# Loading and multiplying the last expert's gate and up rows ahead of the preceding expert's down rows

## The chip, the cores and the metric

One NeuronCore of one Trainium2 chip runs the kernel. The metric is the device time of one execution in microseconds (us); three executions of the kernel before have a median of 1208.63 us (1207.80 to 1209.83). A core has a matrix engine (TensorE, "PE" in the profile, its weight loads "PEld"), a vector engine (VectorE, "DVE"), a scalar engine (ScalarE, "ACT"), a general engine (GpSimd, "POOL") and a queue that issues transfers (SyncE, "SP"). Each engine works through a queue of its own; semaphores make one wait for another.

## The reference

One layer of a trunk: three parallel mixers, then an expert-choice mixture of experts, then a final RMSNorm. The change lies in the last two:

```python
def expert_choice_ffn(h, w_router, w_gate, w_up, w_down):
    b, n, d = h.shape
    cap = CAPACITY_FACTOR * n // N_EXPERTS
    aff = jax.nn.softmax((h @ w_router).astype(jnp.float32), axis=-1)
    gate, idx = lax.top_k(jnp.swapaxes(aff, 1, 2), cap)
    bidx = jnp.arange(b)[:, None, None]
    xe = h[bidx, idx]
    hid = jax.nn.silu(jnp.einsum('becd,edf->becf', xe, w_gate)) * jnp.einsum('becd,edf->becf', xe, w_up)
    ye = jnp.einsum('becf,efd->becd', hid, w_down) * gate[..., None].astype(h.dtype)
    return jnp.zeros_like(h).at[bidx, idx].add(ye)
...
    return rms_norm(x, g_final)
```

There are 512 tokens of 1024 channels and 16 experts. Each expert takes 64 tokens through a gate matrix, an up matrix (both 1024 x 1024) and a down matrix (1024 x 1024), all in float32: 12 MB of weights for each expert.

## The kernel before

**Order of work.** The helper class at lines 61 to 69 keeps the instructions of TensorE, VectorE, ScalarE and GpSimd in program order wherever `pinned[0]` is true. Line 1328 sets it and nothing clears it before line 1692, so through all the experts and the tail each of these engines works in the order in which the code names the instructions.

**Weights.** The expert weights come as chunks of 1 MB: chunk b (0 to 3) of a matrix holds the rows of steps k = 2b and 2b+1 of the products. The list `chunks` (lines 1106 to 1112) fixes the order of loading: for each expert e, first chunk 0 of gate and up of expert e+1, then the four down chunks of e, then chunks 1 to 3 of gate and up of e+1. Below, G15.2 is chunk 2 of the gate matrix of expert 15, U is up and D is down; the last two experts are e = 14 and e = 15. `fetch` (line 1114) issues the next chunk on SP into a free one of 18 buffers; `use` (line 1137) returns a buffer to the free list at the second step of a chunk. The products take the chunks in the order in which they were loaded. One chunk of the 18 is loaded as two halves (line 1131), and so is the very last chunk, D15.3.

**One expert** (lines 1574 to 1639). At the start of iteration e the gate and up products of e stand in two PSUM banks (`og[e]`). They are copied out (`gu`, one half on ScalarE, one on VectorE), TensorE turns them (8 transposes), ScalarE takes the Silu (`sgl`) and VectorE multiplies (`hid`). Between these, TensorE has steps 0 and 1 of the gate and up products of the next expert (`gate_up`, line 1536, eight matmuls a step). Then come the down products (line 1599, 8 steps of 4 matmuls), their weighting (`tt`, on VectorE) and the splitting of the result into a high and a low part (`yh` on ScalarE, `yl` on VectorE, two of each). Then steps 2 to 7 of the next expert's gate and up products.

**Putting tokens back.** Experts go back to their tokens in pairs: `slot_rows` (line 1458) makes four one-hot tiles on VectorE, `slots` (line 1511) turns them with four transposes and three copies on ScalarE into `OT`, and `scatter` multiplies. For the last pair (14 and 15) the one-hots are made at step 2 and turned at step 3 of `gate_up(15, k)`, and the products are left to the tail. `carry` (line 1532) brings the accumulated stream of one token tile and half into a PSUM bank by a product with the identity, so that the last pair's products can be added there: four of these lie at steps 3, 4, 5 and 6 of `gate_up(15, k)` (`EARLY`, line 1546), two behind the down products of expert 15.

**Tail** (lines 1643 to 1692). `last_scatter` adds the last pair to the four token tiles. Six of the eight halves stand in PSUM (carried): ScalarE squares and sums them (`ss3`). Two halves, of tiles 2 and 3, are added on VectorE and squared by `own_square`. The reciprocal root goes in steps on GpSimd (tile 0, then tiles 2 and 3 together) or on VectorE with one power on GpSimd (tile 1), and `put` scales the tile and writes it out.

Of the kernel before, what the change touches and what calls it, by code (L numbers as in the profile page):

```python
# [49 lines left out]
def kernel(ctx, tc, x, c, cctx_x, c_ctx, w_mod, b_mod, g_mix, g_ffn, w_in, decay, ret_gn, w_ret,  # L50
# [20 lines left out]
    def dap(t, offset, ap):  # L71
        return bass.AP(tensor=t.tensor, offset=t.offset + offset, ap=ap)
# [17 lines left out]
    def u8(shape, dtype=F32, name="u8"):  # L90
        return U8p.tile(list(shape), dtype, name=name, tag="u8")
# [32 lines left out]
    def small(shape, name, bufs=1):  # L124
        return keep.tile(list(shape), F32, name=name, tag=name, bufs=bufs)
# [976 lines left out]
    def gate_chunks(e, b0, b1):  # L1102
        for b in range(b0, b1):
            chunks.extend([("G", e, b), ("U", e, b)])

    gate_chunks(0, 0, KT // 2)
    for e in range(NE):
        if e + 1 < NE:
            gate_chunks(e + 1, 0, AHEAD // 2)
        chunks.extend(("D", e, b) for b in range(KT // 2))  # L1110
        if e + 1 < NE:
            gate_chunks(e + 1, AHEAD // 2, KT // 2)

    def fetch(most=99):
        while free and len(loaded) < len(chunks) and most:
# [342 lines left out]
    def slot_rows(e0):  # L1458
        oh = h2(F32R, "oh", (P, TT, P))
        for t in range(TT):  # L1460
            one_hot(oh[:, t, :], t, e0, 2)
        return oh
# [48 lines left out]
    def slots(oh):  # L1511
        o = px()
        for t in range(TT):
            PE.transpose(o[:, t * P:(t + 1) * P], f32(oh[:, t, :]), ident)
        OT = [h2(F32R, name="OT") for _ in range(2)]
        A.activation(OT[0], o, AF.Copy)
        A.activation(OT[1][0:64], o[64:128], AF.Copy)
        A.activation(OT[1][64:128], o[0:64], AF.Copy)
        return OT

# [11 lines left out]
    def carry(t, dh, bank):  # L1532
        Z[t][dh] = bank()
        mm(Z[t][dh], ident, acc(t, slice(dh * 512, dh * 512 + 512)), True, False)

    def gate_up(e, k):
        if k == 0:
            og[e] = [pa(), pa()]
        w = (use("G", e, k), use("U", e, k))
        for f in range(2):  # L1540
            for s_ in range(2):
                mm(og[e][f][64 * s_:64 * s_ + 64, :], xe(k, e), w[s_][:, f * 512:(f + 1) * 512], k == 0, k == KT - 1)
        fetch()

    Z = [[None, None] for _ in range(TT)]
    EARLY = {3: (0, 0, pa), 4: (0, 1, pa), 5: (3, 0, OC), 6: (1, 0, px)}

    ohs = h2(name="ohs", shape=(P, TT, CAP))
    xe0 = h2(name="xe0", shape=(P, KT, CAP))
# [24 lines left out]
    for e in range(NE):  # L1574
        last, par, nx = e == NE - 1, e % 2, e + 1
        gu = [h2(name="gu") for _ in range(2)]
        A.activation(gu[0], og[e][0], AF.Copy)
        V.tensor_copy(gu[1], og.pop(e)[1])
        if not last:
            gate_up(nx, 0)  # L1580
        hid = h2(name="hid", shape=(P, KT, CAP))
        for f in range(2):
            o = px()
            for j in range(4):
                PE.transpose(o[:, j * P:(j + 1) * P], gu[f][:, ch(j)], ident)
            ov = o.rearrange("p (j s) -> p j s", j=4)
            sgl = h2(name="sgl", shape=(P, 4, CAP))
            A.activation(sgl, ov[:, :, 0:CAP], AF.Silu)
            V.tensor_tensor(hid[:, 4 * f:4 * f + 4, :], sgl, ov[:, :, CAP:], op=OP.mult)
        if not last:  # L1590
            gate_up(nx, 1)
        if par and not last:
            oh = slot_rows(e - 1)
        if not par and not last and nx < NE - 1:
            g_ = gather(nx // 2 + 1)
            next(g_)
            next(g_)
        o = px()
        for f in range(KT):
            w = use("D", e, f)  # L1600
            for dh in range(2):
                g = dh ^ par
                mm(o[64 * g:64 * g + 64, :], hid[:, f, :], w[:, dh * 512:dh * 512 + 512], f == 0, f == KT - 1)
            fetch()
        if par == 0:
            Y[e] = [[h2(F32R, name="yy") for _ in range(2)] for _ in range(2)]
        tt = h2(name="tt")
        V.scalar_tensor_tensor(tt, o, gcol[:, e:e + 1], m5[par], op0=OP.mult, op1=OP.mult)
        for g in range(2):
            dh = g ^ par  # L1610
            sl = slice(64 * g, 64 * g + 64)
            yh, yl = Y[e - par]
            A.activation(yh[dh][sl], tt[sl], AF.Copy)
            V.tensor_tensor(yl[dh][sl], tt[sl], f32(yh[dh][sl]), op=OP.subtract)
        if last:
            carry(1, 1, pa)
            carry(2, 0, pa)
            break
        for k in range(AHEAD, KT):
            gate_up(nx, k)  # L1620
            if not par and nx < NE - 1 and k == 4:
                next(g_)
            if par:
                if k == 2:
                    OT = slots(oh)
                elif k < 7:
                    scatter(e - 1, OT, k - 3)
            if nx == NE - 1:
                if k == 2:
                    gfj = u8([P, 2, D], name="gf")  # L1630
                    gf, jka = gfj[:, 0, :], gfj[:, 1, 0:512]
                    SY.dma_start(gf, dap(g_final, 0, [[0, P], [1, D]]))
                    oh = slot_rows(e)
                if k == 3:
                    OT = slots(oh)
                if k in EARLY:
                    carry(*EARLY[k])
        if par:
            Y.pop(e - 1)
    Y = [Y[NE - 2]]  # L1640
# [3 lines left out]
    ss3, rs3 = small([P, 2, TT], "ss3"), small([P, TT], "rs3")  # L1644
    ots = [u8([P, 2, D], name="ot") for _ in range(2)]

    def last_scatter(t):
        ts = slice(t * P, (t + 1) * P)
        for dh in (1, 0):
            carried = Z[t][dh] is not None  # L1650
            z = Z[t][dh] if carried else px()
            mm(z, OT[dh][:, ts], Y[0][0][dh], not carried, False)
            mm(z, OT[dh][:, ts], Y[0][1][dh], False, True)
            if carried:
                A.activation(jka, z, AF.Square, accum_out=ss3[:, dh, t:t + 1])
            else:
                a_ = Z[t][dh] = acc(t, slice(dh * 512, dh * 512 + 512))
                V.tensor_tensor(a_, z, a_, op=OP.add)

    def own_square(t):  # L1660
        A.activation(jka, Z[t][1], AF.Square, accum_out=ss3[:, 1, t:t + 1])

    def last_rsqrt(ta, n):
        G.tensor_tensor(ss3[:, 0, ta:ta + n], ss3[:, 0, ta:ta + n], ss3[:, 1, ta:ta + n], op=OP.add)
        rsqrt(rs3[:, ta:ta + n], ss3[:, 0, ta:ta + n], 1.0 / D, n, G)

    def put(t, helped=()):
        ot = ots[t // 2][:, t % 2, :]
# [6 lines left out]
                V.scalar_tensor_tensor(ot[:, sl], Z[t][dh], rs3[:, t:t + 1], gf[:, sl], op0=OP.mult, op1=OP.mult)  # L1675
            SY.dma_start(dap(out, t * P * D + dh * 512, [[D, P], [1, 512]]), ot[:, sl])

    for t in range(TT):
        last_scatter(t)
    last_rsqrt(0, 1)  # L1680
    own_square(2)
    own_square(3)
    v1 = small([P, 2], "v1")
    V.tensor_tensor(v1[:, 0:1], ss3[:, 0, 1:2], ss3[:, 1, 1:2], op=OP.add)
    v1 = rsqrt_start(rs3[:, 1:2], v1[:, 0:1], 1.0 / D, 1, V)
    put(0)
    rsqrt_end(rs3[:, 1:2], v1, 1, V)
    last_rsqrt(2, 2)
    put(1)
    put(2)  # L1690
    put(3, (0,))
# [76 lines left out]
```

## Time and profile before

| | |
|---|---|
| median of 3 executions | 1208.63 us |
| the profiled execution's own time | 1206.07 us |
| its span | 1204.3 us |
| TensorE busy | 1140.5 us (95%) |
| VectorE busy | 614.4 us (51%) |
| ScalarE busy | 403.9 us (34%) |
| GpSimd busy | 87.2 us (7%) |
| read from HBM | 280.33 MB |
| chain that ended last | TensorE 67%, transfers 22%, VectorE 6%, ScalarE 2% |

The profile is one execution, seen from the inside. Times in it count from the span's start. In a timeline row stand start, duration, engine, line, operation, what is written from what, the shape, and how many instructions the row merges; a bracket gives the time that the engine was idle before and who released it. Line L67 is the helper that orders instructions, so that operations are told apart by the names of their tiles. Neighbouring matmuls overlap in the records, so that a merged row counts longer than its share of the chain. The chain of waits starts from the last instruction and goes back at each step to what released it.

### The profile page before, as it was taken

How to read it: one execution, taken by the hardware profiler on the slowest of the kernel's cores; microseconds unless marked ns; L12 is line 12 of the kernel's file. 1: busy time of each engine (PE TensorE's matmuls, PEld its weight loads, DVE VectorE, ACT ScalarE, POOL GpSimd, SP SyncE). 2: the span in 40 equal slices, each digit the busy share in tenths (PEclk: the TensorE clock that was granted, in tenths of full speed). 3: DMA queues.
4: the chain of work that ended last, by engine and by line, in shares of the span. 5: the costliest groups of instructions: out<-in, count | busy, mean ns of one | idle time of the engine just before them, and what ended most of it. 6: DMA issues, size and time to landing. Idle time of an engine off the chain costs nothing.

```text
span 1204.3 us, 15433 instructions
## 1 busy us (share of the span) xinstructions
PE 1140.5 (95%) x5884; PEld 724.2 (60%) x5884; DVE 614.4 (51%) x1381; ACT 403.9 (34%) x779; POOL 87.2 (7%) x150
## 2 busy tenths in 40 slices
PE   4999999899999999999999979999998998999996
PEld 2788888677678877888888844333333333433332
DVE  3778666588877664686646352233332232223223
ACT  4553334566655444232333232112111111111112
POOL 2011111100032220000000000000000000000001
PEclk9999999999999999999999979999999999999998
DMA  9922122110021215897636467999999999999994
GB/s 273 276 73 70 37 66 76 53 36 19 19 71 36 62 62 200 266 285 236 202 91 258 161 259 264 412 420 420 420 420 419 420 422 420 419 422 419 421 420 160
DMA packets 133669, 285.52 MB, mean 237 GB/s; under 512 B 7702, under 2 KB 97114, under 8 KB 110428
## 3 DMA queue, kind: packets, MB, share of 16 engines
q1 hardware_dynamic: 131868, 278.25, 62.0%
q0 software_dynamic: 1152, 4.19, 0.9%
q10 hardware_dynamic: 576, 2.10, 0.4%
q8 instruction: 46, 0.75, 0.3%
q14 instruction: 27, 0.22, 0.1%
HBM read 280.33 MB, written 4.19 MB: 236 GB/s over the span
## 4 chain that ended last, share of the span: by engine, by line
PE 67%; DMA 22%; DVE 6%; ACT 2%; SPq 1%; POOL 1%; issue 1%; DVEq 0%; POOLq 0%; ACTq 0%
PE px L128 29%; PE pa L67 11%; DMA rg<-in_w_exp_up_dram 10%; PE px L67 9%; PE pa L128 7%; DMA rg<-in_w_exp_gate_dram 6%; DMA rg<-in_w_exp_down_dram 5%; PE PV L128 3%; PE oc L128 3%; PE pa L966 1%; PE pa L1052 1%; PE oy L128 1%; DMA wm<-in_w_mod_dram 1%; DVE rt L455 1%; SPq L240 0%
## 5 line engine op out<-in xcount | busy, mean ns | idle before, releaser
L128 PE MATMUL px<-hx,ws 128*128 128x512 f32 x1344 | 367.6, 398 | 0.0
L67 PE MATMUL pa<-rg,xe 128*64 128x512 f32 x1024 | 259.1, 613 | 19.4 <-DMA rg<-in_w_exp_up_dram 16.2
L128 PEld LDWEIGHTS px<-hx,ws 128*128 128x128 f32 x1344 | 243.3, 189 | 42.9 <-issue 3.1
L67 PEld LDWEIGHTS pa<-rg,xe 128*64 128x64 f32 x1024 | 76.0, 138 | 154.1 <-issue 107.4
L67 PE MATMUL px<-rg,hid 128*64 128x512 f32 x512 | 113.3, 595 | 0.1
L128 PE MATMUL oc<-hc,ws 128*128 128x256 f32 x384 | 85.5, 283 | 0.0
L67 PEld LDWEIGHTS px<-rg,hid 128*64 128x64 f32 x512 | 35.7, 137 | 69.6 <-issue 66.2
L304 DVE TENSOR_TENSOR ws<-rw,ws 128x1024 fp32r<-128x1024 f32 x55 | 67.3, 1225 | 17.0 <-ACT ws L303 16.8
L128 PEld LDWEIGHTS oc<-hc,ws 128*128 128x128 f32 x384 | 69.6, 189 | 9.4 <-DVE vt L525 0.3
L67 DVE TENSOR_TENSOR acc<-px,acc 128x512 f32<-128x512 f32 x58 | 37.4, 686 | 72.4 <-PE px L67 72.4
L67 DVE SCALAR_TENSOR_TENSOR tt<-px,gcol,m 128x512 f32<-128x512 f32 x16 | 12.0, 750 | 110.0 <-PE px L67 110.0
L303 ACT ACTIVATE ws<-rw 128x1024 fp32r<-128x1024 f32 x55 | 57.9, 1054 | 24.8 <-PE px L128 16.3
L67 ACT ACTIVATE yy<-tt 64x512 fp32r<-64x512 f32 x32 | 20.1, 628 | 126.9 <-DVE tt L67 126.5
L128 PE MATMUL px<-yh,ws 128*128 128x512 f32 x192 | 62.5, 392 | 0.0
L922 ACT ACTIVATE Sx<-Sx,nm 128x512 f32<-128x512 f32 (+1 forms) x64 | 47.8, 747 | 30.9 <-DVE nm L958 15.5
L137 DVE TENSOR_TENSOR ws<-rw,ws 128x512 fp32r<-128x512 f32 (+1 forms) x32 | 26.3, 822 | 37.7 <-ACT ws L136 37.6
L67 ACT ACTIVATE gu<-pa 128x512 f32<-128x512 f32 x16 | 9.5, 596 | 104.2 <-PE pa L67 104.2
L67 DVE TENSOR_SCALAR xe<-px,af,sf 128x128 f32<-128x128 f32 (+1 forms) x36 | 14.0, 402 | 58.9 <-ACT xe L67 41.2
L1177 DVE SCALAR_TENSOR_TENSOR mac<-mw,cpad,mac 128x1024 f32<-128x1024 f32 x30 | 38.5, 1282 | 7.6 <-DMA mw<-in_w_mod_dram 7.1
L128 PEld LDWEIGHTS px<-yh,ws 128*128 128x128 f32 x192 | 36.1, 188 | 7.7 <-ACT ws L303 0.2
L128 PE MATMUL pa<-ws,mg 128*128 128x512 f32 x168 | 39.8, 394 | 0.0
L67 ACT ACTIVATE xe<-px,sf,af 128x128 f32<-128x128 f32 (+1 forms) x36 | 15.4, 449 | 66.1 <-PE px L67 58.4
(367 smaller groups left out, 1588.4 us busy)
## 6 DMA issues: line engine op xcount, KB each, us to landing
rg<-in_w_exp_up_dram SPq DMA_DIRECT2D x64, 1024.0 KB, 18.6
rg<-in_w_exp_gate_dram SPq DMA_DIRECT2D x59, 1024.0 KB, 18.7
rg<-in_w_exp_down_dram SPq DMA_DIRECT2D x58, 1024.0 KB, 18.6
rw<-in_w_in_dram SPq DMA_DIRECT2D x58, 512.0 KB, 3.7
mw<-in_w_mod_dram SPq DMA_DIRECT2D x16, 1024.0 KB, 6.8
wm<-in_w_mod_dram SPq DMA_DIRECT2D x16, 512.0 KB, 7.3
rg<-in_w_exp_down_dram SPq DMA_DIRECT2D x12, 512.0 KB, 18.6
rg<-in_w_exp_gate_dram SPq DMA_DIRECT2D x10, 512.0 KB, 18.7
```

The lines of the kernel that those rows point to most:

```text
L67: return (lambda *a_, **k_: tc.keep_in_program_order(f(*a_, **k_))) if pinned[0] else f
L128: PE.matmul(o, lhsT, rhs, start=start, stop=stop)
L137: V.tensor_tensor(lo, src, f32(hi), op=OP.subtract)
L303: A.activation(hi, raw, AF.Copy)
L304: V.tensor_tensor(lo[:, :NV], raw[:, :NV], f32(hi[:, :NV]), op=OP.subtract)
L455: V.tensor_copy(t2[b:b + q], o[c:c + q])
L922: A.activation(Sx[:, :n], Sx[:, :n], AF.Exp, scale=-1.0, bias=nm, accum_out=l[:, 0:1])
L966: PE.transpose(o[:, j * P:(j + 1) * P], SXs[b, j][:, ti * P:(ti + 1) * P], ident)
L1052: PE.transpose(o[:, b * P:(b + 1) * P], SXs[a, b][:, ti * P:(ti + 1) * P], ident)
L1177: V.scalar_tensor_tensor(macs[w], tiles[i], cpad[:, k, 0:1], macs[w], op0=OP.mult, op1=OP.add)
```

## The change

It has four parts. For the last expert alone, all eight gate and up chunks are listed ahead of the down chunks of expert 14, and all its gate and up steps are multiplied ahead of the down products of expert 14. The four early `carry` products move from the gate and up steps into the down products: after steps 3, 5 and 7 of expert 14 and after step 2 of expert 15. The one-hots of the last pair, their turning and the load of `g_final` move behind the down products of expert 14 and the splitting of its result. In the tail, the two halves of token tile 0 are no longer squared on ScalarE: VectorE takes their statistics, works out the mean of squares (the variance plus the square of the mean), and does the root's steps that GpSimd did, with the power still on GpSimd; the steps are placed between the tail's other VectorE work.

```diff
     for e in range(NE):
+
+        some = AHEAD // 2 if e + 1 < NE - 1 else KT // 2
         if e + 1 < NE:
-            gate_chunks(e + 1, 0, AHEAD // 2)
+            gate_chunks(e + 1, 0, some)
         chunks.extend(("D", e, b) for b in range(KT // 2))
         if e + 1 < NE:
-            gate_chunks(e + 1, AHEAD // 2, KT // 2)
+            gate_chunks(e + 1, some, KT // 2)
...
-    EARLY = {3: (0, 0, pa), 4: (0, 1, pa), 5: (3, 0, OC), 6: (1, 0, px)}
+    EARLY = {(NE - 2, 3): (0, 0, pa), (NE - 2, 5): (0, 1, pa), (NE - 2, 7): (3, 0, OC), (NE - 1, 2): (1, 0, px)}
...
         if not last:
-            gate_up(nx, 1)
+            for k in range(1, KT if nx == NE - 1 else AHEAD):
+                gate_up(nx, k)
...
             fetch()
+            if (e, f) in EARLY:
+                carry(*EARLY[e, f])
...
             break
+        if nx == NE - 1:
+            gfj = u8([P, 2, D], name="gf")
+            gf, jka = gfj[:, 0, :], gfj[:, 1, 0:512]
+            SY.dma_start(gf, dap(g_final, 0, [[0, P], [1, D]]))
+            OT = slots(slot_rows(e))
+            continue
         for k in range(AHEAD, KT):
             gate_up(nx, k)
...
-            if nx == NE - 1:
-                if k == 2:
-                    gfj = u8([P, 2, D], name="gf")
-                    gf, jka = gfj[:, 0, :], gfj[:, 1, 0:512]
-                    SY.dma_start(gf, dap(g_final, 0, [[0, P], [1, D]]))
-                    oh = slot_rows(e)
-                if k == 3:
-                    OT = slots(oh)
-                if k in EARLY:
-                    carry(*EARLY[k])
...
+    st0, mv0 = small([P, 2, 6], "st0"), small([P, 2], "mv0")
...
-            if carried:
-                A.activation(jka, z, AF.Square, accum_out=ss3[:, dh, t:t + 1])
-            else:
+            if not carried:
                 a_ = Z[t][dh] = acc(t, slice(dh * 512, dh * 512 + 512))
                 V.tensor_tensor(a_, z, a_, op=OP.add)
+            elif t == 0:
+                V.bn_stats(st0[:, dh, :], z)
+            else:
+                A.activation(jka, z, AF.Square, accum_out=ss3[:, dh, t:t + 1])
...
-    for t in range(TT):
-        last_scatter(t)
-    last_rsqrt(0, 1)
+    last_scatter(0)
+    V.bn_aggr(mv0, st0)
+    v0, v1 = small([P, 1], "v0"), small([P, 2], "v1")
+    V.tensor_tensor(v0, mv0[:, 0:1], mv0[:, 0:1], op=OP.mult)
+    V.tensor_tensor(v0, v0, mv0[:, 1:2], op=OP.add)
+    v0 = rsqrt_start(rs3[:, 0:1], v0, 1.0, 1, V)
+    last_scatter(1)
+    last_scatter(2)
+    rsqrt_end(rs3[:, 0:1], v0, 1, V)
+    last_scatter(3)
     own_square(2)
     own_square(3)
-    v1 = small([P, 2], "v1")
     V.tensor_tensor(v1[:, 0:1], ss3[:, 0, 1:2], ss3[:, 1, 1:2], op=OP.add)
     v1 = rsqrt_start(rs3[:, 1:2], v1[:, 0:1], 1.0 / D, 1, V)
     put(0)
     rsqrt_end(rs3[:, 1:2], v1, 1, V)
-    last_rsqrt(2, 2)
+    G.tensor_tensor(ss3[:, 0, 2:4], ss3[:, 0, 2:4], ss3[:, 1, 2:4], op=OP.add)
+    rsqrt(rs3[:, 2:4], ss3[:, 0, 2:4], 1.0 / D, 2, G)
```

## Rows read from the trace of the kernel before

**Rows 1.** The page, 40 slices of the span: rate of the transfers.
```profile
GB/s 273 276 73 70 37 66 76 53 36 19 19 71 36 62 62 200 266 285 236 202 91 258 161 259 264 412 420 420 420 420 419 420 422 420 419 422 419 421 420 160
```

**Rows 2.** The chain of waits, from 1080 us to the end: start, length, what.
```profile
1112.52 19.81 DMA rg<-in_w_exp_up_dram
...
1155.14 6.87 PE px L67 x32
...
1172.14 1.06 PE oc L67 x2
...
1179.59 7.11 PE px L67 x32
...
1186.73 0.76 DVE tt L67
```

**Rows 3.** SP's timeline, the issues of U15.1 and of D15.3.
```profile
1144.83 0.33 SPq L1133 DMA_DIRECT2D rg<-in_w_exp_up_dram  x1
...
1162.28 2.77 SPq L1131 DMA_DIRECT2D rg<-in_w_exp_down_dram  x2
```

**Rows 4.** The waits of SP, from 1040 us: total, times, longest.
```profile
SPq L1131 <- DMA rg<-in_w_exp_up_dram: 6.2, 3, 2.1
```

**Rows 5.** Stretches: length, PE, PEld, DVE, ACT, POOL busy, TensorE clock, DMA share, GB/s.
```profile
725.00:727.00 2.00, 2.00 (x8) 0.37 (x4) 0.01 (x1) 0.00 (x0) 0.00 (x0) 0.67 0.00 0
1132.30:1133.30 1.00, 0.92 (x4) 0.32 (x5) 0.00 (x0) 0.00 (x0) 0.00 (x0) 0.59 1.02 426
1182.50:1183.00 0.50, 0.50 (x4) 0.14 (x2) 0.00 (x0) 0.00 (x0) 0.00 (x0) 1.00 0.04 16
```

**Rows 6.** Timeline of expert 14's result, the last pair's one-hots, and expert 15's first copy.
```profile
1162.06 0.75 DVE L67 SCALAR_TENSOR_TENSOR tt<-px,gcol,m 128x512 f32<-128x512 f32 x1 [7.91 <-PE px L67]
...
1164.94 0.90 DVE L67 TENSOR_TENSOR oh<-cs,pos 128x128 fp32r<-128x128 f32 x4
1165.84 0.66 PE L67 MATMUL px<-cs,oh 128*128 128x128 f32 x4
...
1166.87 1.80 ACT L67 ACTIVATE OT<-px 128x512 fp32r<-128x512 f32 x3 [2.74 <-PE px L67]
...
1177.24 0.60 ACT L67 ACTIVATE gu<-pa 128x512 f32<-128x512 f32 x1 [8.57 <-PE pa L67]
```

**Rows 7.** Timeline of TensorE around pauses: idle time before the row in brackets.
```profile
720.14 3.68 PE L67 MATMUL px<-ohs,acc 128*128 128x64 f32 x16 [0.99 <-DVE ohs L67]
...
922.96 1.93 PE L67 MATMUL pa<-rg,xe 128*64 128x512 f32 x6 [1.37 <-DMA rg<-in_w_exp_up_dram]
...
1129.89 1.07 PE L67 MATMUL pa<-rg,xe 128*64 128x512 f32 x2 [0.54 <-DMA rg<-in_w_exp_gate_dram]
1132.38 3.60 PE L67 MATMUL pa<-rg,xe 128*64 128x512 f32 x6 [1.41 <-DMA rg<-in_w_exp_up_dram]
```

**Rows 8.** Timeline of the tail, 1186 us to the end.
```profile
1188.17 1.40 DVE L67 TENSOR_TENSOR yy<-tt,yy 64x512 fp32r<-64x512 f32 x2 [0.69 <-ACT yy L67]
...
1195.45 0.19 POOL L67 TENSOR_TENSOR ss<-ss 128x2 f32<-128x2 f32 x1 [1.37 <-ACT gf L67]
...
1197.84 0.75 DVE L67 SCALAR_TENSOR_TENSOR ot<-pa,rs,gf 128x512 f32<-128x512 f32 x1 [0.65 <-POOL rs L67]
1198.51 2.41 DVE L67 SCALAR_TENSOR_TENSOR ot<-acc,rs,gf 128x512 f32<-128x512 f32 x2
1198.61 1.77 POOL L67 TENSOR_TENSOR ot<-ot,gf 128x512 f32<-128x512 f32 x1 [0.80 <-DMA out_dram<-ot]
```

**Rows 9.** Groups by shape, tail and an earlier statistic: busy, mean ns, idle before.
```profile
L67 ACT ACTIVATE gf<-pa 128x512 f32<-128x512 f32 x4 | 2.4, 598 | 0.8 <-PE pa L67 0.7
...
L67 DVE TENSOR_TENSOR acc<-px,acc 128x512 f32<-128x512 f32 x2 | 1.4, 692 | 2.2 <-PE px L67 2.2
...
L67 DVE TENSOR_TENSOR rs_t<-rs 128x1 f32<-128x1 f32 x1 | 0.1, 149 | 0.0
...
L883 DVE BATCH_NORM_STATS2 st<-pa 128x6 f32<-128x128 f32 x16 | 4.0, 274 | 0.0
```

More of the change, by code (lines that the diff above doesn't have):

```diff
@@ L1618 @@
             break
+        if nx == NE - 1:
[4 more added lines that the diff above has]
+            continue
         for k in range(AHEAD, KT):
             gate_up(nx, k)
-            if not par and nx < NE - 1 and k == 4:
+            if not par and k == 4:
                 next(g_)
@@ L1653, in last_scatter @@
             mm(z, OT[dh][:, ts], Y[0][1][dh], False, True)
-            if carried:
-                A.activation(jka, z, AF.Square, accum_out=ss3[:, dh, t:t + 1])
-            else:
+            if not carried:
                 a_ = Z[t][dh] = acc(t, slice(dh * 512, dh * 512 + 512))
                 V.tensor_tensor(a_, z, a_, op=OP.add)
+            elif t == 0:
+                V.bn_stats(st0[:, dh, :], z)
+            else:
+                A.activation(jka, z, AF.Square, accum_out=ss3[:, dh, t:t + 1])
     def own_square(t):
         A.activation(jka, Z[t][1], AF.Square, accum_out=ss3[:, 1, t:t + 1])
-    def last_rsqrt(ta, n):
-        G.tensor_tensor(ss3[:, 0, ta:ta + n], ss3[:, 0, ta:ta + n], ss3[:, 1, ta:ta + n], op=OP.add)
-        rsqrt(rs3[:, ta:ta + n], ss3[:, 0, ta:ta + n], 1.0 / D, n, G)
     def put(t, helped=()):
```

## The prediction

> **What bounds the kernel now.** First the page's slices: from about 750 us on the transfers run at 420 GB/s, slice after slice, until the last one [rows 1]. In that stretch the weights set the pace, and a chunk of 1 MB (1.049 million bytes) takes 1.049 / 0.42 = 2.50 us. Then the chain of waits, to see where this ends. Its last piece that is a transfer ends at 1112.52 + 19.81 = 1132.33 [rows 2]; from there TensorE alone carries the chain to the last down product, which ends at 1186.70, where expert 15's weighting (tt) starts at 1186.73 [rows 2]. The stretches say that the weights have all but landed by 1183.0: the transfer share is 0.04 from 1182.50 [rows 5]. So TensorE ends some 3.7 us behind the last weights. That is the most that any order of these products could win, less what must follow the last chunk: its two steps are 8 of 32 products that take 6.87 together [rows 2], 1.7 us. About 2 us stand to be won, and only if TensorE never waits for anything else.
>
> **Up to the change.** The order of loading differs from the first six chunks after U15.0 on, and so does the order of the products after step 1 of expert 15's gate and up. Nothing before that moves. The transfers stay as they are in number and size, and SP waits there for transfers, not for buffers [rows 4], so the places in the stream keep their landing times. Place by place: the issue of D15.3 at 1162.28 followed the landing of an up chunk [rows 3, 4], which is the one issued eight transfers earlier, U15.1 at 1144.83. In the new order U15.3 has that place. It lands at 1162.26, and D14.0 to D14.3 follow 2.50 apart: 1164.8, 1167.3, 1169.8, 1172.3. D15 keeps its places.
>
> **Expert 15's gate and up, then D14.** Before, D14's products start at 1155.14 [rows 2]; now steps 2 to 7 of expert 15 start there. 48 products at 6.87 / 32 = 0.215 us each take 10.3 us. Step 6 would begin at 1162.0 and waits 0.25 for U15.3, so they end at 1165.7. D14's 32 products follow (6.87), with two of the carries in between, 1.06 each [rows 2]: 1165.7 + 6.87 + 2.12 = 1174.7. No step meets its chunk late: step 4 starts at 1170.2 against 1169.8, step 6 at 1173.0 against 1172.3. Call this end X = 1174.7. The third carry runs to 1175.8.
>
> **What then stands in the way.** Here is the cost of the change. Before, the one-hots of the last pair and their turning lay among expert 15's products, and TensorE had work beside them. Now they stand between D14 and D15 in every queue, and the kernel keeps program order there.
> - VectorE: the one-hots are queued behind tt and the split of D14's result. From tt's start to the end of the fourth one-hot the trace has 1164.94 + 0.90 - 1162.06 = 3.78 us [rows 6]. With 0.04 from the last product to tt: X + 3.82 = 1178.5.
> - TensorE: the four transposes wait for the one-hots, and behind them on TensorE stand expert 15's own transposes and D15. It idles from 1175.8 to 1178.5, or to 1177.9 if each transpose follows its own one-hot.
> - ScalarE: the three copies of OT follow, and behind them stands the copy of expert 15's gate half (gu). From the first transpose to the end of the copies: 1166.87 + 1.80 - 1165.84 = 2.83 us [rows 6], or some 0.4 less if the transposes trail the one-hots. The copies end at 1180.9 to 1181.35.
> - Expert 15: from the start of that copy to D15's first product takes 1179.59 - 1177.24 = 2.35 us [rows 2, 6] (copy, transposes, Silu, product). So D15 starts at 1183.3 to 1183.7 instead of 1179.59. All its chunks have landed by then.
> - D15 took 1186.73 - 1179.59 = 7.14 to tt [rows 2]; the carry after step 2 adds 1.06. So tt starts at 1191.5 to 1191.9 instead of 1186.73: **4.8 to 5.2 us late**, taken as 5.0.
>
> **TensorE's clock.** The granted clock fell to half after pauses of 0.54 and 1.41 that lay close together [rows 7]: 0.59 on the stretch from 1132.30 [rows 5], where six products took 3.60 instead of the 1.93 that six took after a single pause of 1.37 [rows 7]. That is 1.67 us lost. Here the pauses are longer: 2.1 to 2.7 before the four transposes of the one-hots, and from their end (1178.5 to 1179.2) to the end of the gu copy (1181.5 to 1182.0) some 2.9, and the work that resumes is D15. Bounds: 0 if the clock stays at 2.4 GHz, as after the 1.37; and half of the longest run at 1.2 GHz after a restart: TensorE resumed at 720.14 [rows 7], and the stretch 725 to 727 still shows 0.67, two thirds of it at half [rows 5], so until about 726.3, 6.2 us, of which half is lost: 3.1. I take **1.6**, next to the row whose pauses are nearest in kind.
>
> **Moves without cost.** The load of g_final stays behind the last chunk on SP, since every chunk is issued earlier in the code; it needs 1.2 us of transfer (512 KB) after 1183 and is first read in the tail, beyond 1193. Without that cover it would cost those 1.2. The carries of the accumulated stream cost TensorE as much as before; the third falls in a pause.
>
> **Tail.** ScalarE loses two of eight squares, 0.60 each [rows 9] and a read of the sum. Before, GpSimd's root for tiles 2 and 3 starts at 1195.45, after the last square, and VectorE waits 0.65 for it before 1197.84 [rows 8]. That wait has a successor: VectorE's own work. From the last split (1188.17 + 1.40 = 1189.57) to 1197.84 it has 8.27 us. In the changed order it has in that place two statistics, fourteen small operations of 0.15, two additions of 0.69 [rows 9] and four scalings of 0.75 [rows 8]: with a statistic at 0.69, as the additions that read 128x512 from PSUM, 1.4 + 2.1 + 1.4 + 3.0 = 7.9, and with some 0.02 between instructions 8.3. So the tail stays as long as it was: 0. For the statistic the trace shows 0.274 at 128x128 [rows 9]; at 0.27 VectorE is free 0.8 sooner and the root, some 0.5 sooner, sets the start; at four times 0.274 it is 0.8 late.
> A second unknown is the end: of two scalings from SBUF that take 2.41 together, one runs beside GpSimd's product of 1.77 and is the longer by far [rows 8]; alone each would take near 0.75, so this meeting costs 0.9. It could vanish (-0.9) or hit both (+0.9); I leave it as it is. The Trainium skill (SBUF — State Buffer, Who interferes with whom) has a rule for it: a VectorE instruction with two SBUF inputs and a GpSimd one that reads SBUF exclude each other for the whole instruction, whichever starts first. The 2.41 agrees with it. By that rule the meeting would move to where GpSimd's earlier product overlaps a scaling that reads PSUM, and the sum would be about 0.4 us lower. Without it, the tail has **0, from -0.9 to +0.9**.
>
> **Sum.** 5.0 + 1.6 + 0 = +6.6 on the profiled execution's own 1206.07 (span 1204.3 and 1.8 around it): 1212.7. The median of the three runs lies 2.56 above that execution, so 1208.63 + 6.6 = **1215.2 us**, 0.55% slower. Ends: 4.8 + 0 - 0.9 = +3.9 and 5.2 + 3.1 + 0.9 = +9.2, that is 1212.5 and 1217.8.
>
> **Rivals.**
> 1. Not slower: the one-hots run early. VectorE is idle for 7.91 us before expert 14's tt [rows 6], and the one-hots need only positions that are long known. If VectorE took them in that stretch, the transposes would follow the third carry at 1175.8, expert 15's eight transposes behind them (0.66 and about 1.2), and D15 would start near 1178.5, 1.1 early, which its carry eats: tt at 1186.7, 1208.6 us. It decides if the one-hots end before 1175.8. Against it: in the trace they were as ready, and still ran after the split [rows 6]. Chance 0.08.
> 2. Faster: expert 15's activations are made while D14 runs. Its gate and up are complete at 1165.7, nine us before X. With D15 ready as D15.0 lands (1174.8), the end follows the last chunk: 1182.9 + 1.1 = 1184.0 instead of 1186.7, 1205.9 us. It decides if the copy of gu ends before X. Against it: on ScalarE that copy stands behind the copies of OT, which cannot start before 1178. Chance 0.06.
> 3. Slower, but the clock stays up: each pause alone would be near those that the clock outlived [rows 7]. 5.0 + 0: 1213.6 us. For it: a part of the work falls between the two pauses. Against: 0.54 and 1.41 were enough. Chance 0.2.
> The forecast, both pauses and the clock, has 0.66.
>
> **The numbers.** Forecast and rival 3 together 0.86: slower. Differences under 0.2% (2.4 us) cannot be told from none in this kernel; rival 1 is inside, 0.08; rival 2 outside, 0.06. The range takes in both slower cases and the ends above, with 0.5 for the scatter of runs: 1212.0 to 1218.3.
>
> **What would show it.** Right: tt of expert 14 near 1174.8, one-hots until 1178.5, the OT copies before the gu copy on ScalarE, D15 from about 1183.5, a granted clock near 0.5 at its start, tt of expert 15 near 1193, and transfers done at 1183 as before. Wrong: one-hots ahead of expert 14's tt, the gu copy ahead of OT's, or a TensorE without pauses between 1175 and 1184. If D14 itself waits for its chunks, X is wrong, and everything behind moves with it.

## The result, and the profile after

Four executions of the changed kernel have a median of 1216.12 us (1214.25 to 1217.63), four of the kernel before that ran beside them 1208.76. The ratio is 1.0063, with a 95% interval of 1.0050 to 1.0076: **slower by 7.4 us**, where 1215.2 and +6.6 had been forecast.

| | before | after |
|---|---|---|
| the profiled execution's own time | 1206.07 us | 1215.14 us |
| its span | 1204.3 us | 1213.4 us |
| TensorE busy | 1140.5 us | 1141.1 us |
| VectorE busy | 614.4 us | 616.4 us |
| ScalarE busy | 403.9 us | 402.6 us |
| read from HBM | 280.33 MB | 280.33 MB |
| chain that ended last | TensorE 67%, transfers 22% | TensorE 65%, transfers 24% |

Work and traffic are the same; what is new is waiting. The two profiled executions lie 9.07 apart, more than the medians, so the first thing to look for is a difference that the change did not make. It is there, early on. The tile `om` (key products, some 650 us ahead of the first expert) gives it away. Its view has one line for the matmuls: shortest, median and longest duration in ns, then when the first and the last of them start. Kernel before:

```profile
L67 PE MATMUL om<-hx,wk x24: 388/392/520, 29.9 to 64.6; 128*128 128x512 f32 x24
```

Kernel after:

```profile
L67 PE MATMUL om<-hx,wk x24: 387/393/796, 29.7 to 66.7; 128*128 128x512 f32 x24
```

The code up to there is the same, yet the last of them starts 2.1 us later and one takes 796 ns. This delay is carried on to the experts: their first product starts at 720.14 before [rows 7] and at 722.14 after. In the eleven profiles of this study that start scatters from 720.14 to 722.95, whatever the kernel. So all times below are also given **from that start**, as "own stretch", which takes this scatter out: from the start to expert 15's weighting (tt) 466.6 before and 473.8 after, and to the end of the span 484.2 and 491.3. The change costs 7.1 us by this measure. It does not remove all scatter: a second execution of the old order (the second experiment) has 467.8 instead of 466.6.

Now the chain of waits of the kernel after, from the last transfer on (start, length, what), which answers to [rows 2]:

```profile
1147.04 17.41 DMA rg<-in_w_exp_up_dram
1164.49 3.22 PE pa L67 x13
...
1177.47 0.76 DVE tt L67
...
1180.35 0.30 DVE oh L67
...
1180.79 0.86 PE px L67 x4
...
1182.01 0.60 ACT OT L67
...
1183.83 0.61 ACT gu L67
1184.48 1.14 PE px L67 x4
...
1186.54 9.42 PE px L67 x34
1195.98 0.76 DVE tt L67
```

Before, the chain ran on TensorE from the last transfer to expert 15's tt [rows 2], but for 0.9 us between 1178.68 and 1179.59, in which it passes expert 15's Silu and product (chain of the kernel before):

```profile
1178.70 0.39 ACT sgl L67
...
1179.12 0.43 DVE hid L67
```

Now it leaves TensorE at 1177.47, goes through VectorE (weighting, split, one-hots), four transposes, three copies on ScalarE, the copy `gu`, and comes back for D15 at 1186.54 only. The timeline of the kernel after shows how long TensorE and ScalarE stood for it (answers to [rows 6]; idle time before a row in brackets):

```profile
1164.49 3.22 PE L67 MATMUL pa<-rg,xe 128*64 128x512 f32 x13 [1.07 <-DMA rg<-in_w_exp_up_dram]
...
1177.47 0.75 DVE L67 SCALAR_TENSOR_TENSOR tt<-px,gcol,m 128x512 f32<-128x512 f32 x1 [22.76 <-PE px L67]
...
1180.35 0.90 DVE L67 TENSOR_TENSOR oh<-cs,pos 128x128 fp32r<-128x128 f32 x4
...
1180.79 0.84 PE L67 MATMUL px<-cs,oh 128*128 128x128 f32 x4 [2.32 <-DVE oh L67]
...
1182.01 1.80 ACT L67 ACTIVATE OT<-px 128x512 fp32r<-128x512 f32 x3 [2.47 <-PE px L67]
1183.83 0.60 ACT L67 ACTIVATE gu<-pa 128x512 f32<-128x512 f32 x1
...
1184.48 1.98 PE L67 MATMUL px<-cs,gu 128*128 128x128 f32 x8 [2.85 <-ACT gu L67]
...
1186.54 3.89 PE L67 MATMUL px<-rg,hid 128*64 128x512 f32 x12
```

The bank that `gu` copies had been complete since 1168. It was copied at 1183.83, because three copies that could not start before 1182 stood ahead of it on ScalarE. TensorE waits 2.32 for the one-hots and 2.85 for `gu`, where [rows 6] show one-hots and transposes among other products.

The stretches of the kernel after show the third part of the loss (columns as in [rows 5]):

```profile
1187.00:1188.00 1.00, 1.00 (x4) 0.23 (x2) 0.34 (x1) 0.00 (x0) 0.00 (x0) 0.50 0.00 0
1188.00:1189.00 1.00, 1.00 (x6) 0.25 (x4) 0.00 (x0) 0.00 (x0) 0.00 (x0) 0.60 0.00 0
1189.00:1190.00 1.00, 1.00 (x8) 0.27 (x4) 0.00 (x0) 0.00 (x0) 0.00 (x0) 1.00 0.00 0
```

After the two pauses D15 starts at half clock (0.50, 1.2 GHz), four matmuls in a microsecond instead of eight, and gets the full one shortly before 1189 (2.4 GHz, 1.00 from there).

### The profile page after: what moved, and what is told of

Read it like the earlier page. It is cut to its first block, busy times and chain, and to the rows that moved or that the text cites. A ratio compares the mean times of both kernels' runs of the same rounds, so it can differ in the third digit from the quotient of the medians.

```text
span 1213.4 us, 15432 instructions
## 1 busy us (share of the span) xinstructions
PE 1141.1 (94%) x5884; PEld 726.0 (60%) x5884; DVE 616.4 (51%) x1391; ACT 402.6 (33%) x775; POOL 86.1 (7%) x144
## 3 DMA queue, kind: packets, MB, share of 16 engines
HBM read 280.33 MB, written 4.19 MB: 234 GB/s over the span
## 4 chain that ended last, share of the span: by engine, by line
PE 65%; DMA 24%; DVE 6%; ACT 2%; SPq 1%; issue 1%; POOL 1%; DVEq 0%; ACTq 0%; POOLq 0%
PE px L128 28%; DMA rg<-in_w_exp_up_dram 14%; PE pa L67 10%; PE px L67 8%; PE pa L128 7%; DMA rg<-in_w_exp_gate_dram 5%; DMA rg<-in_w_exp_down_dram 3%; PE PV L128 3%; PE oc L128 3%; PE pa L966 1%; PE pa L1052 1%; PE oy L128 1%; DMA wm<-in_w_mod_dram 1%; DVE rt L455 1%; PE om L67 1%
## 5 line engine op out<-in xcount | busy, mean ns | idle before, releaser
L67 PE MATMUL pa<-rg,xe 128*64 128x512 f32 x1024 | 255.0, 606 | 23.1 <-DMA rg<-in_w_exp_up_dram 20.9
L67 PE MATMUL px<-rg,hid 128*64 128x512 f32 x512 | 115.9, 600 | 0.1
```

Of the source, the lines that this page charges most:

```text
L67: return (lambda *a_, **k_: tc.keep_in_program_order(f(*a_, **k_))) if pinned[0] else f
```

## The experiments

The nine runs in a table; the times from the start of the experts are those of each run's profile, the median and ratio those of all its executions. The spans are known to 0.1 us, so differences of the tails under 0.1 say nothing. Each ratio is to executions of the kernel before that ran beside the run, whose medians lie between 1208.63 and 1209.21.

| run | start of experts to tt of 15 | tt of 15 to end | median | ratio to before (95%) |
|---|---|---|---|---|
| before | 466.6 | 17.57 | 1208.76 | |
| after | 473.8 | 17.42 | 1216.12 | 1.0063 (1.0050 to 1.0076) |
| e1_order_only | 474.5 | 17.49 | 1216.42 | 1.0061 (1.0044 to 1.0078) |
| e2_tail_only | 467.8 | 17.39 | 1208.83 | 0.9997 (0.9987 to 1.0007) |
| e3_onehots_early | 470.2 | 17.34 | 1212.14 | 1.0029 (1.0019 to 1.0039) |
| e4_filled_pauses | 473.7 | 17.36 | 1213.27 | 1.0034 (1.0022 to 1.0047) |
| e7_fuller_pauses | 472.6 | 17.36 | 1213.00 | 1.0042 (1.0026 to 1.0058) |
| e5_hidden_early | 466.9 | 17.34 | 1207.52 | 0.9992 (0.9982 to 1.0003) |
| e6_hidden_early_late_carries | 464.5 | 18.01 | 1207.32 | 0.9987 (0.9978 to 0.9995) |
| e8_before_late_carries | 465.8 | 17.99 | 1207.79 | 0.9992 (0.9980 to 1.0003) |
| e9_late_carries_new_tail | 464.6 | 18.05 | 1205.87 | 0.9977 (0.9963 to 0.9990) |

### The new order alone

The changed kernel with the tail of the kernel before:

```diff
-            if not carried:
+            if carried:
+                A.activation(jka, z, AF.Square, accum_out=ss3[:, dh, t:t + 1])
+            else:
                 a_ = Z[t][dh] = acc(t, slice(dh * 512, dh * 512 + 512))
                 V.tensor_tensor(a_, z, a_, op=OP.add)
-            elif t == 0:
-                V.bn_stats(st0[:, dh, :], z)
...
-    last_scatter(0)
-    V.bn_aggr(mv0, st0)
...
+    for t in range(TT):
+        last_scatter(t)
+    last_rsqrt(0, 1)
```

> The changed order of the last two experts with the tail of the kernel before. Theory (the one-hots, their turning and the gu copy stand in the queues between the down products of experts 14 and 15, and the clock falls in the pauses): the whole loss is here, +6 to +9 us on the kernel before, 1215 to 1218; the weighting of expert 15 some 18.5 us after that of expert 14. Rival (the new tail costs the time): back to within 2 us of the kernel before.

It took 1216.42 us, and its tt of experts 14 and 15 lie 18.58 apart (1178.83 and 1197.41). The whole loss comes from the order.

### The new tail alone

The reverse: the kernel before with the tail of the kernel after.

```diff
-            if carried:
-                A.activation(jka, z, AF.Square, accum_out=ss3[:, dh, t:t + 1])
-            else:
+            if not carried:
                 a_ = Z[t][dh] = acc(t, slice(dh * 512, dh * 512 + 512))
                 V.tensor_tensor(a_, z, a_, op=OP.add)
+            elif t == 0:
+                V.bn_stats(st0[:, dh, :], z)
...
+    last_scatter(0)
+    V.bn_aggr(mv0, st0)
...
-    last_rsqrt(2, 2)
+    G.tensor_tensor(ss3[:, 0, 2:4], ss3[:, 0, 2:4], ss3[:, 1, 2:4], op=OP.add)
+    rsqrt(rs3[:, 2:4], ss3[:, 0, 2:4], 1.0 / D, 2, G)
```

> The order of the kernel before with the changed tail. Theory: the tail is worth 0, the time is within 1.5 us of the kernel before (1207.3 to 1210.3), and the stretch from expert 15's weighting to the end of the span stays at 17.4 to 17.6 us. Rival (the new tail costs the time): +5 us or more.

1208.83 us, ratio 0.9997: nothing that can be measured. In the profile the tail is 17.39 long instead of 17.57. So the tail does not cause the loss, and no gain of it can be measured.

This run is also a second look at the old order, and its TensorE timeline has a wait that the profile of before lacks:

```profile
1161.94 1.02 PE L67 MATMUL pa<-rg,xe 128*64 128x512 f32 x2
1164.03 3.65 PE L67 MATMUL pa<-rg,xe 128*64 128x512 f32 x14 [1.07 <-DMA rg<-in_w_exp_up_dram]
```

Here TensorE waits 1.07 for U15.1, in an order in which the profile of before shows no such wait. Counted from the start of the experts U15.1 lands 1.2 later than there (1164.03 - 720.72 = 443.31 against 1162.26 - 720.14 = 442.12). So the landing of the weights against the products scatters by about a microsecond. A prediction that reads a landing time from one execution carries that with it.

### The one-hots early

Of the changed kernel only the one-hots and their turning move, into the gate and up steps of expert 15:

```diff
                 gate_up(nx, k)
+                if nx == NE - 1 and k == 2:
+                    oh = slot_rows(e)
+                if nx == NE - 1 and k == 3:
+                    OT = slots(oh)
...
-            OT = slots(slot_rows(e))
```

> The changed kernel with the one-hots made after step 2 and turned after step 3 of expert 15's gate and up, as in the kernel before; the order of weights and products stays the changed one. Theory: ScalarE reaches the gu copy right behind the split of expert 14's result, 2.1 us after its last product, expert 15's down products start some 4.5 us after it instead of 9, the single pause of some 1.7 us leaves the clock up: 5 to 6 us less than the changed kernel, 1209.5 to 1211.5. Rival (the loss comes with the new order of the weights, which arrive late for expert 14's down products): no better than the changed kernel, 1214 or more.

1212.14 us, 4.0 less than after, and 0.6 above the expected range. The first half of the expectation held: D15 starts 4.47 after expert 14's tt (1182.82 against 1178.35). The timeline of TensorE in this run shows one pause left, for the copy of `gu`:

```profile
1181.15 0.74 PE L67 MATMUL px<-cs,gu 128*128 128x128 f32 x4 [1.79 <-ACT gu L67]
1182.12 0.72 PE L67 MATMUL px<-cs,gu 128*128 128x128 f32 x4 [0.24 <-DVE gu L67]
1182.82 4.49 PE L67 MATMUL px<-rg,hid 128*64 128x512 f32 x12
```

And its stretches show what had not been expected:

```profile
1182.00:1183.00 1.00, 0.88 (x6) 0.74 (x8) 0.42 (x1) 0.43 (x2) 0.00 (x0) 1.00 0.90 361
1183.00:1184.00 1.00, 1.00 (x4) 0.26 (x4) 0.42 (x1) 0.26 (x1) 0.00 (x0) 0.51 0.72 291
1184.00:1186.00 2.00, 2.00 (x6) 0.49 (x4) 0.00 (x0) 0.00 (x0) 0.00 (x0) 0.50 0.31 123
```

The transposes still run at the full clock; then, with TensorE busy, it falls to half and stays there beyond 1186. Twelve products take 4.49, and D15 with its carry 10.04 where 8.2 had been expected. In this execution one pause of 1.79 and one of 0.24 had come before. So moving the one-hots saves about 4, and by this profile what remains of the loss is the pause for `gu` and the clock.

### The pauses filled

To price the clock by itself: the queues stay as in the changed kernel, but TensorE gets products to do in the two pauses, whose result nobody reads. The variant e4_filled_pauses has two products of 512 columns in each; e7_fuller_pauses, shown here, has two and a half and three.

```diff
+    def idle_work(*ns):
+        z = px()
+        for n in ns:
+            mm(z[:, :n], ident, acc(0, slice(0, n)), True, True)
...
-            OT = slots(slot_rows(e))
+            oh = slot_rows(e)
+            idle_work(512, 512, 256)
+            OT = slots(oh)
+            idle_work(512, 512, 512)
             continue
```

> The changed kernel with two products of the identity in each of the two pauses, into a bank that nobody reads, some 2.1 us each time, which leave every wait in place. Theory: the granted clock stays at 1.0 when expert 15's down products start, they take 8.2 us with their carry instead of 9.4, and the kernel gains 1.6 us on the changed one, 1214 to 1215. Rival (the clock costs nothing, all of the loss is the waits): no gain, or up to 1 us lost.

> The changed kernel with idle products that fill the two pauses more fully than in the first try (two and a half before the one-hots' transposes, three before expert 15's), whose remaining pauses of 0.6, 1.1 and 0.45 us still let the clock fall. Theory: the clock stays up, expert 15's down products take 8.2 us to the weighting instead of 9.4 to 10, the stretch from the first product of the experts to that weighting is 472.3 instead of 473.9. Rival (the clock falls with the pause before the down products alone, or the products lost to it are not what costs): the stretch stays at 473.6 or grows.

With two products the pauses shrink to 0.59, 1.13 and 0.45. TensorE's timeline of e4_filled_pauses:

```profile
1178.63 0.84 PE L67 MATMUL px<-cs,oh 128*128 128x128 f32 x4 [0.59 <-DVE oh L67]
...
1182.33 1.23 PE L67 MATMUL px<-cs,gu 128*128 128x128 f32 x8 [1.13 <-ACT gu L67]
1184.00 4.49 PE L67 MATMUL px<-rg,hid 128*64 128x512 f32 x12 [0.45 <-DVE hid L67]
```

Twelve products again take 4.49: against the expectation the clock fell, though later than in the changed kernel. There the eight transposes of `gu` ran at half clock already (1.98), here they take 1.23. From the start of the experts to tt this run needs 473.7, as after does. Its median is 2.9 lower than that of after, and the profile does not say why; its own experts started 1.8 earlier (720.36), and the median may hold some of that scatter. Whether the clock fell in its other executions too is not known. For the price of the clock this run decides nothing.

With the fuller pauses the clock holds in the profile. TensorE's timeline of e7_fuller_pauses:

```profile
1179.12 0.84 PE L67 MATMUL px<-cs,oh 128*128 128x128 f32 x4 [0.16 <-DVE oh L67]
...
1182.82 1.23 PE L67 MATMUL px<-cs,gu 128*128 128x128 f32 x8 [0.27 <-ACT gu L67]
1184.49 2.80 PE L67 MATMUL px<-rg,hid 128*64 128x512 f32 x12 [0.45 <-DVE hid L67]
```

and a stretch of the same run:

```profile
1186.00:1188.00 2.00, 2.00 (x9) 0.44 (x4) 0.00 (x0) 0.00 (x0) 0.00 (x0) 1.00 0.00 0
```

The same twelve products take 2.80. From the end of D14 (1175.76) to tt of expert 15 (1192.84) it is 17.08, against 18.56 in the changed kernel: by these two profiles the clock costs 1.5 us there. The rest of the loss stays with TensorE kept busy and at full clock: 6.0 against before's 466.6, 4.8 against the 467.8 of the second look at its order. That is the wait in the queues, as the theory had it. The medians do not confirm this price: by the ratios this run gains 2.5 us on after, and e4_filled_pauses, in whose profile the clock did fall, 3.5; the intervals of the two overlap. That the fuller pauses are why the clock held is not shown either: elsewhere the same pauses came with the one and the other (last section).

### Expert 15's activations during D14

If the queues are the cause, the loss goes once nothing stands between D14 and D15. On top of the early one-hots, expert 15's copies, transposes, Silu and product come while D14 runs; two carries go between the products of D15.

```diff
+            if nx == NE - 1:
+                gu_last = gate_copies(nx)
+                hid_last = h2(name="hid", shape=(P, KT, CAP))
...
             fetch()
+            if nx == NE - 1 and f in (1, 3):
+                hidden(hid_last, gu_last, f // 2)
...
-    EARLY = {(NE - 2, 3): (0, 0, pa), (NE - 2, 5): (0, 1, pa), (NE - 2, 7): (3, 0, OC), (NE - 1, 2): (1, 0, px)}
+    EARLY = {(NE - 2, 5): (0, 0, pa), (NE - 2, 7): (0, 1, pa), (NE - 1, 2): (3, 0, OC), (NE - 1, 4): (1, 0, px)}
```

> The kernel of the one-hots-early run, and also expert 15's gu copies ahead of the down products of expert 14, and its transposes, Silu and product between their steps; the carries of (3,0) and (1,0) at steps 2 and 4 of expert 15's down products. Nothing of the last pair or of expert 15's activations then stands between the two sets of down products. Theory (the loss is that queue of work, not the order of the weights): TensorE has no pause there, expert 15's weighting comes some 1 us earlier than in the kernel before, counted from the first product of the experts (466.6 there, 473.9 in the changed kernel), and the time is 1206.5 to 1209. Rival (expert 14's down products, late in the stream, keep the time up): 1211 or more.

1207.52 us: 8.6 less than after, and no different from before (0.9982 to 1.0003). TensorE has no pause from step 2 of expert 15 to tt. So all of the loss is undone by moving the vector and scalar work, with the weights in the order of the change. The time is within what was expected, the stretch to tt is not: 466.9, as long as before's 466.6, where about 1 less had been expected. Two carries, 2.12 us, still lie between the products of D15, at 1180.93 and 1183.86, when all other work is done.

### The carries moved into the tail

The two carries go into the tail, each right ahead of the scatter products that need it; the tail is that of the kernel before.

```diff
-    EARLY = {(NE - 2, 5): (0, 0, pa), (NE - 2, 7): (0, 1, pa), (NE - 1, 2): (3, 0, OC), (NE - 1, 4): (1, 0, px)}
+    EARLY = {(NE - 2, 5): (0, 0, pa), (NE - 2, 7): (0, 1, pa)}
+    LATE = {(1, 0): px, (3, 0): OC}
...
         for dh in (1, 0):
+            if (t, dh) in LATE:
+                carry(t, dh, LATE[t, dh])
+            if (t, dh) == (3, 0):
+                own_square(2)
+                own_square(3)
```

> The same with the tail of the kernel before, and the carries of (1,0) and (3,0) taken out of the down products and put into the tail, where TensorE waits for ScalarE's squares; the squares of tiles 2 and 3 that VectorE adds go ahead of that of (3,0). Theory: TensorE reaches the end of the transfers, the weighting of expert 15 comes 2 to 3 us earlier than in the kernel before (464 from the first product), the tail is 0.3 us longer, 1205 to 1207, faster than both kernels. Rival: the two carries cost in the tail what they save (no better than 1208), or the last chunk lands later than 1183 and holds the down products.

1207.32 us, ratio 0.9987 (0.9978 to 0.9995): a little faster than the kernel before, though 0.3 above the expected range. The stretch to tt is 464.5 where 464 had been expected, the tail 0.4 longer. The timeline of this run (TensorE and ScalarE):

```profile
1166.82 0.60 ACT L67 ACTIVATE gu<-pa 128x512 f32<-128x512 f32 x1 [5.73 <-PE pa L67]
...
1169.29 0.74 PE L67 MATMUL px<-cs,gu 128*128 128x128 f32 x4
...
1177.30 1.13 PE L67 MATMUL pa<-acc,cs 128*128 128x512 f32 x2
1178.36 7.09 PE L67 MATMUL px<-rg,hid 128*64 128x512 f32 x32
```

`gu` is copied as soon as its bank is complete, 16 us earlier than in the changed kernel by the count from the start of the experts (1166.82 - 720.98 against 1183.83 - 722.14), and D15 follows the carry at once.

The carries moved on the kernel before, to see what they are worth without the new order:

```diff
-    EARLY = {3: (0, 0, pa), 4: (0, 1, pa), 5: (3, 0, OC), 6: (1, 0, px)}
+    EARLY = {3: (0, 0, pa), 4: (0, 1, pa)}
+    LATE = {(1, 0): px, (3, 0): OC}
...
         for dh in (1, 0):
+            if (t, dh) in LATE:
+                carry(t, dh, LATE[t, dh])
```

> The kernel before, its own order of weights and products, with only the carries of (1,0) and (3,0) moved into the tail as in the fast run. Theory A (the gain of the fast run is the two carries that TensorE no longer does ahead of the last down products; the order of the weights is worth nothing once nothing stands in the way): the weighting of expert 15 comes some 2 us earlier than before, 464.5 to 465 from the first product of the experts, the tail takes 18.0 instead of 17.6, 1206.5 to 1208, level with the fast run. Theory B (the order of the weights gives it): expert 15's last gate and up rows are waited for, the weighting stays at 466 or later, 1208.5 or more.

1207.79 us (0.9980 to 1.0003), as theory A had it; the stretch to tt is 465.8, which lies between the two expectations. TensorE's timeline shows the wait of the second experiment again:

```profile
1165.90 3.65 PE L67 MATMUL pa<-rg,xe 128*64 128x512 f32 x14 [1.08 <-DMA rg<-in_w_exp_up_dram]
```

Against that experiment, with the same wait, the stretch to tt is 2.0 shorter, the two carries; the tail is 0.4 longer than before's (17.99 against 17.57). So the late carries explain a part of the gain. By these profiles the new order with its queues freed gives the rest, 1.3 to tt (464.5 against 465.8). But two executions of the old order differ by as much (466.6 and 467.8), and the ratios of the two kernels, 0.9987 and 0.9992, are too near each other: a gain by the order is not shown.

### The best of both

The sixth kernel with the tail of the kernel after:

```diff
-    for t in range(TT):
-        last_scatter(t)
-    last_rsqrt(0, 1)
+    last_scatter(0)
+    V.bn_aggr(mv0, st0)
...
+    last_scatter(1)
+    last_scatter(2)
+    rsqrt_end(rs3[:, 0:1], v0, 1, V)
+    last_scatter(3)
```

> The fast run with the changed tail (statistics of tile 0 on VectorE) instead of that of the kernel before. Theory: with the late carries ScalarE's squares set the tail, so taking two of them off it gives back 0.3 to 0.6 of the 18.0 us, 1206.5 to 1207.3. Rival: VectorE, with 8.3 us of work ahead of the third tile, or TensorE's late carries keep the tail at 17.8 or more, no change.

1205.87 us, ratio 0.9977 (0.9963 to 0.9990), the fastest of the study. The reason expected for it is not borne out: the tail is 18.05 long, as with the old tail (18.01), and the stretch to the end 482.6 against 482.5. ScalarE reads its last sum, now that of the half of tile 3 carried last, 9.1 to 9.2 after tt with either tail (at 1194.63 and 1194.62), so that the squares taken from it shorten nothing. The lower median is not explained by the profile, and the intervals of the two kernels overlap.

## Why the prediction was right, step by step

The forecast was +6.6 by the queues and the clock. Measured were +7.4 in the medians and +7.1 in the own stretch of the two profiles (+5.9, if the second look at the old order, 467.8 to tt, stands for before). Its steps, with the 2.0 of the late start taken off where absolute times are compared:

- **Landing of U15.3.** Forecast 1162.26, measured 1164.49 - 2.00 = 1162.49. The rule that places in the stream keep their landing times held here, in part by luck: in the second experiment, with the old order, the same place landed at 1164.03 - 0.58 = 1163.45 by this count. The wait was 1.07 instead of 0.25. Two products of step 6 did not need that chunk, and TensorE stood there some 1.0 sooner (1163.42 - 2.00, where the forecast would have the two done at 1162.0 + 0.43): it had not lost the 1.67 by the clock that [rows 7] show at 1132.38. That saved nothing, since the chunk was waited for.
- **X, the end of D14.** Forecast 1174.7, measured 1177.42 - 2.00 = 1175.4. This is the term that was mis-sized, by 0.7. From the landing of U15.3 on there are 46 products and two carries, which at 0.215 and 1.06 make 12.0; they took 12.9 (1164.49 to 1177.42). The 0.215 was taken from a long run, but groups of eight between carries take 1.87 to 1.89 in the chain instead of 1.72, and the eight ahead of the first carry take 2.10 (1169.47 to 1171.57). Their first weight load starts as D14.1 lands, which the forecast had just in time (1167.3 against 1167.4; measured 1169.47 - 2.00 = 1167.47). The weight load in the timeline of the kernel after:

```profile
1169.47 1.22 PEld L67 LDWEIGHTS px<-rg,hid 128*64 128x64 f32 x8 [0.50 <-DMA rg<-in_w_exp_down_dram]
```

So 0.9 came from the products and 0.2 from the later landing, less 0.4 for the two early products.
- **One-hots.** From tt to the end of the fourth, 1180.35 + 0.90 - 1177.47 = 3.78, to the hundredth as in [rows 6].
- **Copies of OT.** They end at 1183.81, 6.39 after D14 (forecast 6.2 to 6.65). The transposes did trail their one-hots, starting 0.44 after the first of them.
- **From the `gu` copy to D15.** 1186.54 - 1183.83 = 2.71 instead of 2.35. The transposes ran at half clock; in the run with the clock held it was 2.32.
- **The clock.** 2.71 - 2.35 = 0.36, and 9.44 - 8.2 = 1.24 in D15 with its carry, together 1.6, the value taken. By the run that held the clock it is 1.5. Rival 3, pauses that leave the clock alone, did not happen in this profile. That the value fits is in part luck: it was taken next to the row of 0.54 and 1.41, and in the kernel after these same two pauses, at the same place, cost nothing (last section).
- **X to tt of expert 15.** All of it together: 18.56 measured, 18.6 forecast (1186.73 + 5.0 + 1.6 - 1174.7).
- **Tail.** Forecast 0, measured -0.15 in the profile and nothing in the median of the second experiment.

The differences add up: 0.7 at X, -0.1 from there to tt, -0.15 in the tail make the 0.5 between +6.6 and +7.1.

The tail is worth a look, since two squares left ScalarE and nothing came of it. The timeline of the kernel after (answers to [rows 8, 9]):

```profile
1198.87 1.30 DVE L67 BATCH_NORM_STATS2 st<-pa 128x6 f32<-128x512 f32 x2
1199.89 0.60 ACT L67 ACTIVATE gf<-pa 128x512 f32<-128x512 f32 x1 [1.84 <-PE pa L67]
...
1204.24 0.19 ACT L67 ACTIVATION_READ_ACCUMULATOR gf<-acc 128x1 f32 x1
1204.50 0.20 POOL L67 TENSOR_TENSOR ss<-ss 128x2 f32<-128x2 f32 x1 [0.59 <-ACT gf L67]
...
1206.24 1.45 DVE L67 SCALAR_TENSOR_TENSOR ot<-pa,rs,gf 128x512 f32<-128x512 f32 x2
...
1207.61 2.41 DVE L67 SCALAR_TENSOR_TENSOR ot<-acc,rs,gf 128x512 f32<-128x512 f32 x2
1207.70 1.77 POOL L67 TENSOR_TENSOR ot<-ot,gf 128x512 f32<-128x512 f32 x1 [0.80 <-ACT ot L67]
```

ScalarE has two squares less, but waits 1.84 for TensorE to finish the third bank: its first square starts 3.91 after tt, and it had started 2.72 after tt before. So its last sum is read only 0.2 earlier than before (8.45 after tt instead of 8.65), and GpSimd's root starts 8.52 after tt, where [rows 8] have 1195.45 - 1186.73 = 8.72. VectorE gets to the last pair of scalings at about the time that the root is there: 1207.61 - 1195.98 = 11.63 after tt, 11.78 before. The prediction named VectorE's own work as the successor; it is that and ScalarE's later start: GpSimd's root ends at 1206.90 and VectorE's preceding scaling at 1206.98.

The statistic was assumed at 0.69 and took 0.690 each in the grouped view (two of them 1.30 in the merged row, since they overlap). The meeting at the end stayed as it was, 2.41 beside 1.77: the scalings and GpSimd's product start 0.09 apart, 0.10 before.

The Trainium skill (SBUF — State Buffer, Who interferes with whom) has such a pair contend for one shared port pair, which it calls an exclusive lock. The chain agrees with that, as far as it goes: the second scaling counts 1.67 from 1208.35 to 1210.02 and ends 0.55 after GpSimd's product (1209.47). The 0.4 that the sum would have been lower by it supposed that the meeting moved, and it did not; no run here holds the two apart.

Rival 1 (one-hots early) and rival 2 (activations during D14) did not happen, for the reason given against them, the order in the queues. Made on purpose they gave less than they were priced at. One-hots made early, at a somewhat earlier place than rival 1 had them, gave 1212.14 where 1208.6 had stood: the price left out the wait for the copy of `gu`, 1.79 and 0.24, and the clock behind it. Rival 2's place (e5_hidden_early) gave 1207.52 where 1205.9 had stood: two carries, 2.12 us, still lay among the products of D15, and with them moved away the stretch to tt was 464.5, where its 1184.0 makes 463.9 (less 720.14).

## What to carry to other kernels

When matmuls are reordered, write down for each engine what its queue holds between the two pieces that now stand next to each other: work that was hidden beside the one is bare between the two, and in a fixed program order one late instruction (here the copies of the one-hots) holds up the next, which had been ready for 15 us. Weights in another order won nothing here that could be measured, where TensorE ended only 3.7 us behind the last of them; what counts after the last weight is what TensorE still has to do that could be done earlier or in the tail. And compare stretches from a common event, since a difference of 2 us at the start of the experts would have passed for a part of the change here.

## What the runs showed of the hardware beyond that

- The same pauses did not always bring the clock down. In the kernel before, 0.54 with 1.41 were followed by six products in 3.60 [rows 7]. The same two pauses at the same place in TensorE's timeline of the kernel after left them at 1.93:

```profile
1132.11 1.07 PE L67 MATMUL pa<-rg,xe 128*64 128x512 f32 x2 [0.54 <-DMA rg<-in_w_exp_gate_dram]
...
1134.59 1.93 PE L67 MATMUL pa<-rg,xe 128*64 128x512 f32 x6 [1.41 <-DMA rg<-in_w_exp_up_dram]
```

Of the eleven profiles two (before and e5) have 3.60 there and nine have 1.93, with pauses of 0.54 to 0.56 and 1.40 to 1.42 in all. So the profiles of the experiments say what happened in one execution each: the clock fell after 1.79 with 0.24 (e3) and after 0.59, 1.13 and 0.45 (e4), and it held with 0.16, 0.27 and 0.45 (e7). That a pause of a certain length is enough, or is not, they do not show. In e3 it fell only about 2 us after TensorE had gone back to work, so that the loss lies in products that wait for nothing.
- Filling the pauses in part brought nothing in the stretch to tt of the one profile (473.7 against 473.8), in which the clock fell all the same.
- Executions of the same code differ by up to 2.8 us in the start of the experts (720.14 to 722.95; between before and after the 2 us arose within the first 67 us), and by 1.5 us in when the same place of the weight stream lands, counted from that start (441.98 in e4, 443.47 in e8). Together this is more than the effect of most experiments here, and only the medians or the own stretch show those.
